# Squares of A's first block moved from the first pass to the third and fifth late pair, B's first squares all on ScalarE, and a new instruction order, in a 4096³ matmul with GELU

## The chip, the cores and the metric

The kernel runs on one core of one Trainium2 chip. The metric is device time in microseconds (us) of one launch. The profiled execution gives each engine's span in addition: TensorE (PE, with its weight loads PEld), VectorE (DVE), ScalarE (ACT), GpSimd (POOL, which issues the loads that cast f32 to f16) and SyncE (SP, which issues the stores).

## The reference

```python
def setup_inputs():
    m, k, n = 4096, 4096, 4096
    return {"a": np.random.randn(m, k).astype(np.float32),
            "b": np.random.randn(k, n).astype(np.float32)}

def reference(a, b):
    x = np.matmul(a, b)
    return 0.5 * x * (1 + np.tanh(np.sqrt(2 / np.pi) * (x + 0.044715 * x**3)))
```

## The kernel before, in words

**Tiling.** The product is computed in f16 with a seven-product scheme (Strassen and Winograd) instead of eight. A and B are cut into quadrants 11, 12, 21, 22. A *group* is one pair (mb, nb): 512 rows of each half of A by 512 columns of each half of B, over the whole depth of 4096; there are 16 groups. Group 0 (`first_group`) computes the first half of its depth with eight plain products, while the inputs still arrive, and the second half with seven. Groups 1 to 3 (`raw_group`, `last_raw`) use seven products P1 to P7. The other twelve groups run as six *late pairs* (`late_pair`, `ga` = 4, 6, 8, 10, 12, 14), where each product is split by the same scheme once more (`split_pair`). The third and fifth late pair are `ga` = 8 and 12. PE runs all products in one fixed sequence.

**Where things lie.** SBUF tiles: `aT` holds the transposed quadrants of A, `bR` eight chunks for quadrants of B and their sums, `aD` four chunks for sums of A, `stage` two chunks for rows as loaded, `y` small f32 blocks, `acc` the eight PSUM banks. In group 0, `bR_73/74` are the two depth halves of B12, `bR_75/76` of B22, `bR_77/78` of B21, `bR_79/80` of B11. Loads of f32 inputs go through POOL's queue and are cast on the way; sums of B that later groups need again are stored by SP (`k_unit`) and fetched by POOL.

**The check.** f16 is only used if no row of A and no column of B is too large or too small: the kernel sums squares of A's rows into `stats["a"]` and of B's columns into `stats["b"]`, and at the end `final_checks` and `verdict` decide whether `general_path` must run. For A's first block the squares are taken as each chunk is loaded in `load_a_`: sixteen `weigh0` activations per chunk (L684, `weigh_row`), written to a junk buffer with the row sum beside it; `weigh_first_half` adds the parts. The later blocks of A are squared in `turn_quad` (L1359, `weigh`). B's squares are 1024-wide pieces: `square` makes them on ACT (L1408) or on DVE (L1405), as the table `SQ` says for the four quadrants of group 0's first half, and DVE adds them up in bf16 (L1413). The pieces go through spare buffers: in group 0 one `y` block and the four halves of `bR_78`, the chunk that B21's second half is loaded into later.

**What sets the order.** All work after the first two products is recorded in a `Plan` as operations with an engine, a cost, what they read and write, and a slack. A planner with a table of costs (`COST`, `EVERY`, `MOVE`, `WEIGHT`) puts each engine's operations in order; `EARLIER` shifts due times of single operations, and `AFTER` is a list of moves "put operation n right behind m" made on the planner's result. Each engine then runs its list strictly in that order, so a waiting instruction holds what stands behind it.

```python
SQ = {"12": True, "11": True, "22": False, "21": True}   # True: on DVE
...
            for r in range(NX):                            # in load_a_, 16 rows of a chunk
                act("weigh0", lambda r=r: weigh_first(quad, cc, (r,), next(junk)), toks,
                    [("w0",), ("rows", 0), ("rows", 1)],
                    batch=("w0", quad, cc), slack=FIRST_SLACK)
```

The line numbers in the profile are those of the kernel; L964 (`combine2`: sums of A or B chunks on DVE), L1322 (`add_bank`: PSUM plus a block), L656 (`transpose`), L838 (`dma`), L744 and L1972 (the products), L1316 and L2384 (copies out of and between banks on ACT) are helpers that many steps share.

Of the kernel before, what the change touches and what calls it, by code (L numbers as in the profile page):

```python
# [18 lines left out]
Q = 32  # L19
# [33 lines left out]
UNDER_WAY = {"POOL": [(0.68, 12.2)] * 4}  # L53
# [2470 lines left out]
```

## Time and profile before

| | |
|---|---|
| median of 3 runs | 1445.19 us (1443.98 to 1448.59) |
| profiled execution, its own time | 1448.0 us |
| its span (first to last instruction) | 1446.4 us |
| PE busy | 1419.4 us, 98% of the span |
| DVE busy | 1238.0 us, 86% |
| ACT busy | 692.1 us, 48% |
| POOL busy | 487.5 us, 34% |
| moved by DMA | 380.99 MB; 339.74 MB read from HBM |

PE works nearly all the time, so what can be gained or lost lies in the few places where it waits, most of them in the first 130 us. The page's busy shares are averages; the stages differ: in group 0 the inputs arrive at about 200 GB/s (counted on the f16 side), and in the late pairs the DMA engines have room.

### The profile page before, as it was taken

What the parts mean: (1) busy time and instruction counts of PE and PEld (TensorE: products, weight loads), DVE (VectorE), ACT (ScalarE), POOL (GpSimd) and SP (SyncE); (2) the same over time, 40 slices, a digit from 0 to 9 for tenths busy, and PEclk for the clock granted to TensorE, in tenths of its full rate; (3) what the DMA queues carried; (4) which work ended last, traced back from release to release, by engine and by line L of the source; (5) the groups of instructions that cost most, each with busy time, mean ns of one, the idle gap of its engine ahead of it and who ended that gap; (6) DMA issues with size and microseconds to landing.
All of it is one profiled execution on the core that took longest, in us unless ns stands there. A gap on an engine that the chain in (4) does not pass through costs nothing. (4 is left out here: it accounts for less than half of the span.)

```text
span 1446.4 us, 19351 instructions
## 1 busy us (share of the span) xinstructions
PE 1419.4 (98%) x6707; PEld 656.3 (45%) x6707; DVE 1238.0 (86%) x1331; ACT 692.1 (48%) x1492; POOL 487.5 (34%) x892
## 2 busy tenths in 40 slices
PE   8989999999999999999999999999999999999998
PEld 3434455465444444444444444444444444444443
DVE  2997797998889999979897988887998998878876
ACT  4966656358866313543655313353463622333133
POOL 6554245054225152324423342332322231231220
PEclk9999999999999999999999999999999999999999
DMA  9999999999999998989979897998998967796773
GB/s 171 203 241 272 311 298 266 338 237 271 295 299 248 335 201 231 310 276 276 321 259 318 274 216 270 257 248 276 280 348 241 302 160 228 273 313 217 260 256 140
DMA packets 207674, 380.99 MB, mean 263 GB/s; under 512 B 20944, under 2 KB 119760, under 8 KB 207568
## 3 DMA queue, kind: packets, MB, share of 16 engines
q0 software_dynamic: 150400, 247.52, 71.7%
q1 hardware_dynamic: 57168, 132.15, 24.4%
q8 instruction: 55, 0.90, 0.2%
q14 instruction: 51, 0.42, 0.1%
HBM read 339.74 MB, written 134.22 MB: 328 GB/s over the span
## 5 line engine op out<-in xcount | busy, mean ns | idle before, releaser
L1972 PE MATMUL acc<-bR 128*128 128x512 f16 x1568 | 346.8, 379 | 0.4 <-DVE bR L964 0.2
L1972 PEld LDWEIGHTS <-bR 128*128 128x128 f16 x1984 | 193.9, 98 | 235.0 <-DVE bR L964 1.3
L1972 PE MATMUL acc<-bR,aT 128*128 128x512 f16 x1280 | 283.4, 379 | 4.8 <-DVE bR L964 3.9
L1972 PEld LDWEIGHTS <-aT 128*128 128x128 f16 x1664 | 162.6, 98 | 202.0 <-issue 6.2
L838 POOL DMA_DIRECT2D bR<-k_unit x224 | 121.4, 545 | 367.9 <-PE acc L1972 265.2
L964 DVE TENSOR_TENSOR bR<-bR 128x4096 f16<-128x4096 f16 (+1 forms) x114 | 210.6, 1858 | 29.6 <-PE acc L1972 20.3
L838 POOL DMA_DIRECT2D bR<-in_b_dram x320 | 173.6, 546 | 159.0 <-DMA bR<-in_b_dram 61.3
L1984 ACT COPY acc<-acc 128x512 f32<-128x512 f32 x168 | 95.7, 574 | 274.7 <-PE acc L1972 247.4
L1322 DVE TENSOR_TENSOR y<-acc,y 128x512 f32<-128x512 f32 x269 | 177.1, 685 | 25.1 <-PE acc L1972 24.2
L1972 PE MATMUL acc<-bR,aD 128*128 128x512 f16 x736 | 163.6, 379 | 0.0
L1296 ACT ACTIVATE y<-y 128x512 f32<-128x512 f32 x174 | 105.3, 625 | 112.2 <-DVE y L1322 111.9
L1972 PEld LDWEIGHTS <-aD 128*128 128x128 f16 x1024 | 100.2, 98 | 120.8
L744 PE MATMUL acc<-bR,aT 128*128 128x512 f16 x544 | 119.9, 379 | 2.2 <-DVE y L1322 1.2
L744 PEld LDWEIGHTS <-aT 128*128 128x128 f16 x768 | 75.1, 98 | 92.3 <-issue 3.3
L1981 ACT COPY y<-acc 128x512 f32<-128x512 f32 x114 | 66.4, 585 | 94.5 <-PE acc L1972 87.1
L1408 ACT ACTIVATE y<-bR 128x1024 bf16<-128x1024 f16 x83 | 84.9, 1051 | 36.5 <-DVE y L1413 33.8
L838 POOL DMA_DIRECT2D stage<-in_b_dram x104 | 56.3, 546 | 121.9 <-PE acc L1045 32.3
L744 PEld LDWEIGHTS <-aD 128*128 128x128 f16 x608 | 59.4, 98 | 77.9 <-DVE aD L964 4.2
L1972 PE MATMUL acc<-stage,bR 128*128 128x512 f16 x416 | 94.0, 379 | 0.0
L1413 DVE TENSOR_TENSOR y<-y 128x1024 bf16<-128x1024 bf16 x102 | 70.0, 688 | 25.6 <-ACT y L1408 24.0
L1972 PE MATMUL acc<-stage,aT 128*128 128x512 f16 x384 | 86.8, 379 | 0.0
L1327 DVE TENSOR_TENSOR acc<-acc,y 128x512 f32<-128x512 f32 x115 | 78.9, 693 | 5.3 <-ACT y L1981 5.0
(128 smaller groups left out, 1769.0 us busy)
## 6 DMA issues: line engine op xcount, KB each, us to landing
bR<-k_unit POOLq DMA_DIRECT2D x224, 512.0 KB, 7.8
out_dram<-y SPq DMA_DIRECT2D x194, 256.0 KB, 6.8
bR<-in_b_dram POOLq DMA_DIRECT2D x328, 128.0 KB, 7.0
k_unit<-bR SPq DMA_DIRECT2D x78, 512.0 KB, 7.0
stage<-k_unit POOLq DMA_DIRECT2D x60, 512.0 KB, 7.0
bR<-in_a_dram POOLq DMA_DIRECT2D x64, 256.0 KB, 9.2
k_unit<-stage SPq DMA_DIRECT2D x30, 512.0 KB, 8.0
out_dram<-bR SPq DMA_DIRECT2D x56, 256.0 KB, 6.7
```

Source lines behind the costliest of these rows:

```text
L744: nc.tensor.matmul(acc, sa[:, j // 2, i * P : (i + 1) * P, j % 2], sb[:, j, :], start=start and j == 0, stop=stop and j == 3, skip_group_c ...
L838: return plan.add(queue, COST[queue], lambda: eng.dma_start(out=dst, in_=src), r=r, w=w, size=MOVE[what] * SPREAD, weight=weight, **kw)
L964: nc.vector.tensor_tensor(out=dst, in0=xa, in1=ya, op=ALU.add if op > 0 else ALU.subtract)
L1296: act("gelu", lambda: nc.scalar.activation(t, t, ACT.Gelu_apprx_tanh), [("f", f)], [("f", f)])
L1322: dve("add", lambda: nc.vector.tensor_tensor(out=sm(g), in0=bank(s, i), in1=sm(f), op=ALU.add), [("f", f)], [("f", g), ("p", s, i)])
L1327: dve("add", lambda: nc.vector.tensor_tensor(out=bank(s, i), in0=bank(s, i), in1=sm(f), op=ALU.add), [("f", f)], [("p", s, i)])
L1408: act("square", lambda t=t, src=src: nc.scalar.activation(t, src, ACT.Square), [c(cx)], [("f", f)], slack=60.0, lead=lead)
L1413: dve("add16", lambda t=t, u=u: nc.vector.tensor_tensor(out=u, in0=u, in1=t, op=ALU.add), [("f", f)], [("f", e)], slack=60.0, lead=lead)
L1972: nc.tensor.matmul(bank(w, i), sa[:, jx // 2, r * P : (r + 1) * P, jx % 2], bv[:, jx, :], start=p in "17" and jx == 0, stop=jx == NJ - 1, ...
L1981: act("copy", lambda: nc.scalar.copy(out=sm(f), in_=bank(w, i)), [("p", w, i)], [("f", f)])
L1984: act("copy", lambda: nc.scalar.copy(out=bank(*dst), in_=bank(*x)), [("p", *x)], [("p", *dst)])
```

## The change

1. `load_a_` and the first steps no longer square A's rows: the 128 `weigh0` activations, `weigh_row`, `weigh_first` and `weigh_first_half` are gone.
2. A new `weigh_again` reads the rows of A's first block a second time: eight sets, each four loads through POOL into a free chunk, eight in-place `weigh` activations, and after every fourth set one small reduction on DVE. `AGAIN` puts the sets at the products P6, P5, P3 and P4 of the late pairs 8 and 12. A gate ties the loads to a PE operation nine before the place in PE's sequence.
3. `SQ` is False for all quadrants: the twelve squares that DVE made in group 0 are made by ACT.
4. `EARLIER`, `AFTER` and the planner's costs are new, so the order of DVE, ACT, POOL and SP changes from the first loads on. PE's sequence of products is the same; from the third late pair on some operands lie in other chunks.

```diff
-UNDER_WAY = {"POOL": [(0.68, 12.2)] * 4}
+UNDER_WAY = {"POOL": [(0.68, 13.2)] * 4}
...
-SQ = {"12": True, "11": True, "22": False, "21": True}
+SQ = {'12': False, '11': False, '22': False, '21': False}
...
+AGAIN = {8: {'P6': ('11', 0), 'P5': ('11', 1), 'P3': ('12', 0), 'P4': ('12', 1)}, 12: {'P6': ('21', 0), 'P5': ('21', 1), 'P3': ('22', 0), 'P4': ('22', 1)}}
+AGAIN_SLACK = 20.0
...
+    def weigh_again(quad, h, x0):
+        ih, kh = int(quad[0]) - 1, int(quad[1]) - 1
+        n = NX // 2
+        s, toks, t = chunk(x0).rearrange("p (x r) -> p x r", r=CH * RUN), [c(x0), c(x0 + 1)], rows_again[ih]
+        gate = [o for o in plan.ops if o.eng == "PE"][-CAST_BACK:][:1]
+        for g in range(4):
+            dma("POOL", s[g * Q : (g + 1) * Q, :, :], a_v[kh, g, :, ih * MH // Q + h * n : ih * MH // Q + (h + 1) * n, :],
+                [], toks, "raw_a", batch=("again", quad, h), slack=AGAIN_SLACK, after=gate)
+        for x in range(n):
+            r = h * n + x
+            act("weigh", lambda x=x, r=r: nc.scalar.activation(
+                s[:, x, :], s[:, x, :], ACT.Square, accum_out=t[:, kh, r : r + 1]),
+                [], [("again", ih), *toks], batch=("wa", quad, h), slack=SLACK)
+        if kh and h:
+            dve("small", lambda: nc.vector.tensor_reduce(
+                out=stats["a"][:, ih * NX : (ih + 1) * NX], in_=t.rearrange("p k x -> p x k"), axis=AX.X, op=ALU.add,
+            ), [("again", ih)], [("sa", 0, ih)], slack=60.0)
...
+        again = dict(AGAIN.get(ga, {}))
+
         def both(name, fresh, done):
+            if name in again:
+                x = new_chunk()
+                weigh_again(*again.pop(name), x)
+                free_cells.extend((x, x + 1))
...
-            for r in range(NX):
-                act("weigh0", lambda r=r: weigh_first(quad, cc, (r,), next(junk)), toks,
-                    [("w0",), ("rows", 0), ("rows", 1)],
-                    batch=("w0", quad, cc), slack=FIRST_SLACK)
...
-        dve("stat", weigh_first_half, [("w0",)], [("sa", 0, 0), ("sa", 0, 1)], slack=300.0)
```

**Loads in group 0.** POOL's queue from the first load of B11's first half (`bR_79`) on, before. `stage_87` receives A21, `stage_86` A12, `aD_82` A22 (first halves); `bR_75` is B22, `bR_77` B21:

```order
L838 DMA bR_79<-in_b_dram 32x4x512 x5
L838 DMA stage_87<-in_a_dram 32x16x256
L838 DMA bR_79<-in_b_dram 32x4x512 x3
L838 DMA stage_87<-in_a_dram 32x16x256
L838 DMA bR_75<-in_b_dram 32x4x512
L838 DMA stage_86<-in_a_dram 32x16x256
L838 DMA stage_87<-in_a_dram 32x16x256 x2
L838 DMA stage_86<-in_a_dram 32x16x256 x2
L838 DMA bR_77<-in_b_dram 32x4x512 x2
```

The same place in the change:

```order
L913 DMA bR_79<-in_b_dram 32x4x512 x8
L913 DMA stage_87<-in_a_dram 32x16x256 x4
L913 DMA stage_86<-in_a_dram 32x16x256
L913 DMA bR_75<-in_b_dram 32x4x512
L913 DMA stage_86<-in_a_dram 32x16x256 x3
L913 DMA bR_77<-in_b_dram 32x4x512 x3
```

All of B11 now goes ahead of A21, and all of A21 ahead of B22 and A12. Further down the queue, before, up to the last load of B21's first half (`bR_77`):

```order
L838 DMA bR_77<-in_b_dram 32x4x512 x2
L838 DMA bR_75<-in_b_dram 32x4x512 x3
L838 DMA aD_82<-in_a_dram 32x16x256 x2
L838 DMA bR_75<-in_b_dram 32x4x512 x4
L838 DMA aD_82<-in_a_dram 32x16x256 x2
L838 DMA stage_87<-in_a_dram 32x16x256 x4
L838 DMA bR_77<-in_b_dram 32x4x512 x4
```

and in the change, where `bR_74` and `bR_80` are second halves of B12 and B11:

```order
L913 DMA bR_80<-in_b_dram 32x4x512
L913 DMA bR_75<-in_b_dram 32x4x512 x4
L913 DMA bR_80<-in_b_dram 32x4x512
L913 DMA bR_74<-in_b_dram 32x4x512 x2
L913 DMA bR_77<-in_b_dram 32x4x512
L913 DMA bR_80<-in_b_dram 32x4x512 x2
L913 DMA bR_77<-in_b_dram 32x4x512 x3
L913 DMA aD_82<-in_a_dram 32x16x256 x4
```

The last load of B21 stood behind eight loads of A22 and of A11's second half; now four loads each of `bR_74` and `bR_80` stand ahead of it instead, and A22 comes behind it.

**DVE in the second half of group 0**, before, up to the transposes of A12's second half (`aT_68`). L1413 are the additions of B's squares:

```order
L1322 TENSOR_TENSOR y_98<-acc_107,y_98 128x512
L1413 TENSOR_TENSOR y_97<-y_97,bR_78 128x1024
L1322 TENSOR_TENSOR y_99<-acc_108,y_99 128x512
L1413 TENSOR_TENSOR y_97<-y_97,y_102 128x1024
L1322 TENSOR_TENSOR y_90<-acc_109,y_90 128x512
L1322 TENSOR_TENSOR y_100<-acc_109,y_100 128x512
L1413 TENSOR_TENSOR y_97<-y_97,bR_78 128x1024
L1413 TENSOR_TENSOR y_96<-y_96,bR_78 128x1024
L1413 TENSOR_TENSOR y_97<-y_97,bR_78 128x1024
L1322 TENSOR_TENSOR y_91<-acc_110,y_91 128x512
L1322 TENSOR_TENSOR y_101<-acc_110,y_101 128x512
L656 STREAM_TRANSPOSE aT_68<-stage_87 128x4x256 x2
```

The same place in the change:

```order
L1039 TENSOR_TENSOR bR_74<-bR_76,bR_74 128x2048
L1397 TENSOR_TENSOR y_98<-acc_107,y_98 128x512
L1039 TENSOR_TENSOR bR_74<-bR_76,bR_74 128x2048
L1039 TENSOR_TENSOR aT_72<-aT_66,aT_72 128x2048
L1397 TENSOR_TENSOR y_91<-acc_110,y_91 128x512
L1397 TENSOR_TENSOR y_89<-acc_108,y_89 128x512
L1397 TENSOR_TENSOR y_90<-acc_109,y_90 128x512
L1397 TENSOR_TENSOR y_99<-acc_108,y_99 128x512
L1397 TENSOR_TENSOR y_100<-acc_109,y_100 128x512
L752 STREAM_TRANSPOSE aT_68<-stage_87 128x4x256
L1397 TENSOR_TENSOR y_101<-acc_110,y_101 128x512
L752 STREAM_TRANSPOSE aT_68<-stage_87 128x4x256
```

No addition of squares is left there. Between the first transpose of `aT_72` and the first of `aT_68` the list held twelve L1413 and two L1405 before, and holds four L1413 (now L1509) in the change; the last of them that reads `bR_78` stands before the second `aD_81` sum.

**Loads in the third late pair.** POOL in the change, around the loads of P3 from the input (`bR_74`, `bR_73`, `stage_87`, `bR_75`); the `in_a_dram` rows are the rows of A read again, `k_unit_241` a cast of B made for a later pair:

```order
L913 DMA bR_73<-in_a_dram 32x8x512 x4
L913 DMA bR_78<-k_unit_218 128x2048
L913 DMA stage_86<-k_unit_234 128x2048 x2
L913 DMA bR_78<-k_unit_218 128x2048
L913 DMA k_unit_241<-in_b_dram 32x4x512
L913 DMA bR_77<-k_unit_218 128x2048
L913 DMA bR_74<-in_b_dram 32x4x512 x2
L913 DMA bR_77<-k_unit_218 128x2048
L913 DMA bR_74<-in_b_dram 32x4x512 x4
L913 DMA bR_73<-in_b_dram 32x4x512 x4
L913 DMA bR_74<-in_b_dram 32x4x512
L913 DMA bR_73<-in_b_dram 32x4x512 x2
```

Before, the queue there held, after the casts and the fetches of P5's sums, only P3's loads:

```order
L838 DMA stage_87<-k_unit_250 128x2048 x2
L838 DMA bR_73<-k_unit_234 128x2048
L838 DMA k_unit_257<-in_b_dram 32x4x512
L838 DMA bR_73<-k_unit_234 128x2048
L838 DMA stage_86<-in_b_dram 32x4x512
L838 DMA bR_75<-k_unit_250 128x2048 x2
L838 DMA stage_86<-in_b_dram 32x4x512 x2
```

Ten loads of A now go ahead of the last of P3's 32 loads, and three of the sixteen casts, all ahead of it before, behind it.

More of the change, by code (lines that the diff above doesn't have):

```diff
@@ L1 @@
 from contextlib import ExitStack
-from itertools import cycle
 import concourse.bass as bass
@@ L60 @@
 MOVE = {
-    "store": 1.345, "fetch": 1.38, "quarter": 1.6, "piece": 1.27, "out": 0.73, "raw_a": 1.3, "raw_b": 0.645,
-    "raw_a0": 1.363, "raw_b0": 0.64, "tiny": 0.2, "out_half": 0.3,
+    "store": 1.31, "fetch": 1.291, "quarter": 1.6, "piece": 1.27, "out": 0.743, "raw_a": 1.304, "raw_b": 0.649,
+    "raw_a0": 1.377, "raw_b0": 0.6444, "tiny": 0.2, "out_half": 0.3,
 }
 WEIGHT = {
-    "raw_a0": 1.31, "raw_b0": 1.06, "store": 2.0, "fetch": 2.42, "quarter": 2.16, "piece": 2.16, "raw_a": 1.11,
-    "raw_b": 1.06, "out": 1.05,
+    "raw_a0": 1.263, "raw_b0": 1.13, "store": 2.06, "fetch": 2.18, "quarter": 2.16, "piece": 2.16, "raw_a": 1.22,
+    "raw_b": 0.98, "out": 1.14,
 }
@@ L299 @@
 LEAD12 = 0.0
+LEAD11 = 500.0
 LEAD22 = 0.0
@@ L680, in load @@
             nc.gpsimd.dma_start(out=dst, in_=src)
-    def weigh_row(dst, src, to=None):
-        nc.scalar.activation(src if to is None else to, src, ACT.Square, accum_out=dst)
-    def weigh_first(quad, c, xs, to=None):
-        ih, kh = int(quad[0]) - 1, int(quad[1]) - 1
-        for x in xs:
-            k = ((kh * CH + c) * 2 + ih) * NX + x
-            weigh_row(stats["a"][:, k : k + 1], staged[quad, c][:, x, :], None if to is None else to[:, :])
-    def weigh_first_half():
-        t = tallies[:, 4 * NX : 6 * NX]
-        nc.vector.tensor_reduce(
-            out=t, in_=stats["a"].rearrange("p (k x) -> p x k", k=2 * CH), axis=AX.X, op=ALU.add
-        )
-        nc.vector.tensor_copy(out=stats["a"][:, : 2 * NX], in_=t)
     def gather(s):
@@ L792, in half_path @@
     before = {}
-    for n, whats in ((0, "A11_0a B12_0a A11_0b B12_0b T11_0a T11_0r T11_0s W11_0"),):
+    for n, whats in ((0, "A11_0a B12_0a A11_0b B12_0b T11_0a T11_0r T11_0s"),):
         for what in whats.split():
             half = what[-1] == "0" and what != "A11_0"
-            if what[0] == "W":
-                before.setdefault(n, []).append((weigh_first, (what[1:3], int(what[4]), range(NX))))
-                continue
             for h in (0, 1) if half else (None,):
@@ L1331, in half_path @@
     next_stage = [0]
-    rows = [tallies[:, 2 * ih * NX : 2 * (ih + 1) * NX].rearrange("p (k x) -> p k x", k=2) for ih in range(2)]
+    rows, rows_again = (
+        [tallies[:, 2 * k * NX : 2 * (k + 1) * NX].rearrange("p (k x) -> p k x", k=2) for k in (2 * n, 2 * n + 1)]
+        for n in range(2)
+    )
     seen_rows = set()
@@ L2316, in first_group @@
         SPARES[0][:] = [14, *spares_1]
-        load_b_("11", 0)
+        load_b_("11", 0, LEAD11)
         load_a_("21", 0)
```

4 lines of the change are left out of this document (2 added, 2 removed), and 416 rows, old and new, of tables (AFTER, EARLIER).

## The prediction

> **What bounds the kernel now.** I read the page first, then the list of whom PE waits for, PE's own timeline at those waits, and then, stage by stage, DVE, POOL and the two DMA queues. The page's span and busy shares:
>
> ```profile
> span 1446.4 us, 19351 instructions
> PE 1419.4 (98%) x6707; PEld 656.3 (45%) x6707; DVE 1238.0 (86%) x1331; ACT 692.1 (48%) x1492; POOL 487.5 (34%) x892
> ```
>
> PE is idle for 1446.4 - 1419.4 = 27.0 us, and PE's sequence of products isn't changed, so the change can gain at most part of these 27 us. The list of PE's waits (us in total, times, longest):
>
> ```profile
> PE acc L2260 <- DMA bR<-in_b_dram: 4.5, 3, 2.9
> PE acc L744 <- DVE aD L964: 4.4, 3, 1.9
> PE acc L1972 <- DVE bR L964: 4.1, 3, 2.4
> PE acc L744 <- DVE stage L964: 2.1, 2, 1.8
> PE acc L773 <- DVE aT L656: 1.6, 1, 1.6
> PE acc L753 <- DVE table L811: 1.5, 1, 1.5
> PE acc L744 <- DVE y L1322: 1.2, 1, 1.2
> PE acc L744 <- ACT acc L2384: 1.0, 1, 1.0
> PE acc L1972 <- DMA bR<-in_b_dram: 0.8, 1, 0.8
> PE acc L1972 <- DMA bR<-k_unit: 0.2, 1, 0.2
> ```
>
> They sum to 21.4 us; the other 5.6 us are the tail behind the last product. L753 and L773 (3.1 us, before the first data are there) keep their order, as does the tail. L2260, aD and ACT acc (9.9 us) are group 0; "stage" (2.1) is group 1; the L1972 rows and y (6.3) come later. PE's timeline, with its wait ahead of each piece in brackets:
>
> ```profile
> 14.87 5.45 PE L773 MATMUL acc<-bR,aT 128*128 128x512 f16 x24 [1.59 <-DVE aT L656]
> 23.20 27.16 PE L2260 MATMUL acc<-bR,aT 128*128 128x512 f16 x118 [2.88 <-DMA bR<-in_b_dram]
> 54.48 20.66 PE L2260 MATMUL acc<-bR,aT 128*128 128x512 f16 x95 [0.95 <-DMA bR<-in_b_dram]
> 115.70 7.07 PE L744 MATMUL acc<-aD,aT 128*128 128x512 f16 x32 [1.17 <-DVE aD L964]
> 180.32 7.07 PE L744 MATMUL acc<-stage,aD 128*128 128x512 f16 x32 [1.85 <-DVE stage L964]
> 863.99 7.08 PE L1972 MATMUL acc<-bR,aT 128*128 128x512 f16 x32 [2.38 <-DVE bR L964]
> ```
>
> **The change, part by part.** *The loads at the start.* PE waits 2.88 us for B11's first half (`bR_79`). Whole loads of A are 262 KB on the f16 side; the two queues in 30 to 80 us carry, in MB and in share of 16 engines:
>
> ```profile
> q0 software_dynamic: 14921, 9.56, 130.1%
> q1 hardware_dynamic: 144, 0.52, 2.8%
> ```
>
> That is 9.56 + 0.52 MB in 50 us, about 0.20 MB per us, so a load of A takes 1.3 us and one of B 0.65 us. One load of A, ahead of the last three of `bR_79` before, now stands behind: the product can start 1.3 us earlier. The wait also cost clock. The stretches behind it (last columns: granted clock, DMA share, GB/s):
>
> ```profile
> 24.00:26.00 2.00, 2.00 (x6) 0.76 (x5) 0.00 (x0) 0.00 (x0) 1.16 (x2) 0.50 1.42 195
> 26.00:28.00 2.00, 2.00 (x10) 0.87 (x9) 0.00 (x0) 0.00 (x0) 0.59 (x2) 0.92 1.44 198
> ```
>
> Half speed from 23.2 to 26 and a little after lost some 1.5 us; the 1.59 us wait at 13.3 lost none. With a wait of 1.6 us I expect none, so 2.8 us in all. The next product needs A21, whose last load has one load of B and one of A less ahead of it, 0.65 + 1.3 = 1.95 us; this caps the gain, so I take 2.0 us (0 if transfers in flight share evenly and nothing lands earlier, 2.8 at most). The Trainium skill ("TensorE: Matmul & The Clock Gate", Part 1) has the clock fall only after an idle window of about 3.4 us; by it the 2.88 us wait would not have lost 1.5 us, and the sum for this place would be 1.3 us; the trace shows the loss.
>
> PE's other two waits for B in group 0 (4.5 - 2.9 = 1.6 us) are for B21's first half: 56 units of 0.65 us stood up to its last load, now 48, which is 5.2 us earlier; 1.6 us go (0 to 1.6). A22, now behind it, comes 12 units (7.8 us) later. Its transposes began here:
>
> ```profile
> 46.51 2.37 DVE L656 STREAM_TRANSPOSE aT<-aD 128x1024 uint32<-128x1024 uint32 x2 [1.33 <-DMA stage<-in_a_dram]
> ```
>
> so they come at about 54, and its product is the one behind the waits that end at 54.5, each product of 32 matmuls taking 7 us: it stays covered by that product, and if the cover goes, up to 1.6 us come back.
>
> *Squares off DVE and ACT in group 0.* DVE in 63 to 111 us (after the window's length stand the busy us of PE, PEld, DVE, ACT and POOL), and the additions of squares among its groups in 30 to 130 us:
>
> ```profile
> 63.00:111.00 48.00, 43.75 (x202) 19.42 (x200) 47.40 (x59) 33.51 (x117) 26.00 (x48) 1.00 1.23 231
> ...
> L1413 DVE TENSOR_TENSOR y<-y,bR 128x1024 bf16<-128x1024 bf16 x18 | 12.1, 683 | 0.2
> ```
>
> DVE is full there (47.4 of 48), and PE's three waits for `aD` lie in it. The order takes 12 + 2 squares and additions in this stretch down to 4: ten instructions of 12.1/18 = 0.67 us, 6.7 us. That covers the 4.4 us of waits. ACT's 128 squares of rows, which stood between its copies, go too:
>
> ```profile
> L684 ACT ACTIVATE stat_b<-stage x40: 399/406/433, 30.0 to 106.9; 128x256 f16<-128x256 f16 x40
> L1408 ACT ACTIVATE bR<-bR x9: 1040/1050/1057, 51.6 to 93.2; 128x1024 bf16<-128x1024 f16 x9
> ```
>
> At least 128 x 0.41 = 52 us leave, 12 x 1.05 = 12.6 us come, so PE's 1.0 us wait for ACT can go. Together 5.4 us (2 to 5.4: sums that now run early may wait for the chunks they need, and hold DVE's list).
>
> The front's sum is 2.0 + 1.6 + 5.4 = 9.0 us at 116 us.
>
> *What the transfers give back.* Group 1's sums wait for the last of its B: DVE at 179 us. POOL in 130 to 190 us waits nearly always for earlier loads to land (us, times, longest). Then the queues' shares in 80 to 180, q1 alone in 183 to 188, and both in 180 to 430 us:
>
> ```profile
> 179.04 1.23 DVE L964 TENSOR_TENSOR stage<-bR,stage 128x2048 f16<-128x2048 f16 x1 [1.80 <-DMA bR<-in_b_dram]
> ```
>
> ```profile
> POOL bR L838 <- DMA bR<-in_b_dram: 16.5, 18, 1.4
> ```
>
> ```profile
> q0 software_dynamic: 12540, 10.69, 67.9%
> q1 hardware_dynamic: 6128, 17.14, 46.6%
> ...
> q1 hardware_dynamic: 568, 2.06, 102.3%
> ...
> q0 software_dynamic: 25834, 25.47, 60.5%
> q1 hardware_dynamic: 15904, 46.31, 49.3%
> ```
>
> A full q0 shows 130% and a full q1 102%. So 80 to 180 us are filled to 67.9/130.1 + 46.6/102.3 = 0.98: 2.3 us are free. Removing squares removes no transfer; the loads group 1 needs, and the stores ahead of them, are the same in number. So of 9.0 us I let PE keep 2.3 us at its product at 180 us; the rest shows up as a longer wait there, now 2.1 us. The bounds are 0 (no free time can be used) and 9.0 (stores slip behind the loads).
>
> *Behind 180 us.* The 6.3 us of later waits are each short of one late chunk or one sum; every list is ordered anew. DMA has 1 - 60.5/130.1 - 49.3/102.3 = 0.05 free in 180 to 430 us. No row prices a new order; between 6.3 us gained and 3 us lost (another wait as long as the 2.38 us at 861 us) I take the half, 3.1 us.
>
> *Rows read again.* 32 loads of 1.3 us are 41 us of transfer, 64 squares, at the durations of the later blocks' squares,
>
> ```profile
> L1359 ACT ACTIVATE stage<-stage x64: 612/617/656, 643.9 to 1144.4; 128x512 f16<-128x512 f16 x64
> L1359 ACT ACTIVATION_READ_ACCUMULATOR stage<-stage x64: 185/189/214, 644.4 to 1144.9; 128x1 f32 x64
> ```
>
> at most 64 x 0.81 = 52 us of ACT, in two of the six late pairs. ACT is 48% busy over the span, and PE's list has no wait for such squares, which ran in the second and fourth pair. POOL issues 32 more loads; it is 34% busy. The cover is thin only where pair 8 waits for P3's loads; DVE there, and the queues in 814 to 864 us:
>
> ```profile
> 861.65 2.29 DVE L964 TENSOR_TENSOR bR<-stage,bR 128x4096 f16<-128x4096 f16 x1 [3.26 <-DMA stage<-in_b_dram]
> ```
>
> ```profile
> q0 software_dynamic: 5998, 8.88, 85.0%
> q1 hardware_dynamic: 1008, 1.84, 9.7%
> ```
>
> 85.0/130.1 + 9.7/102.3 = 0.75, so 12.6 of 50 us are free. Ahead of P3's last load come ten loads of A more (13.0 us) and three casts less (1.9 us): 11.1 us. It fits if spread; I take 0.5 us (0 to 11).
>
> **Sum.** -2.3 - 3.1 + 0.5 = -4.9 us. The profiled execution took 1448.0 us (span 1446.4 and 1.6 around it), 0.2% over the median; from it 1443.1, from the median 1445.2 - 4.9 = **1440.3 us**.
>
> **Rivals.**
>
> 1. *The front's gain stays.* If transfers can overlap better than the shares say, all 9.0 us remain: 9.0 + 3.1 - 0.5 = 11.6, 1433.6 us. For it: some stretches were not full, such as this one, with its 216 GB/s:
>
> ```profile
> 100.00:105.00 5.00, 5.00 (x25) 2.27 (x24) 4.94 (x7) 5.00 (x20) 2.99 (x6) 1.00 1.07 216
> ```
>
> Against it: the fill of 0.98, and POOL waiting for landings 18 times.
> 2. *Nothing stays.* The transfers take back all of the front, and the later waits only change places: 0 to 2 us, about 1444 us. For it: the same fill; group 1 ends when its last load lands. The Trainium skill ("DMA: Bandwidth & Descriptors", Issuing engines are not separate DMA queues) says that DMAs of all issuers end up on the same 16 engines and interleave, so a load issued earlier meets the same stores; here q0 and q1 do add up to one full share.
> 3. *Slower: the rows read again hold up P3 in pair 8.* The ten loads meet P3's in the last part of the stretch up to the sum at 861 us, where only part of the 12.6 us is free. All 11.1 us late in pair 8 and 2 us in pair 12 cost 13, less the 5.4 of front and order: 1452.8 us. It is slower by 0.3% (4.3 us, about what a measurement can tell) only from 9.7 us on, when the 2.4 us wait becomes 12. Against it: eight of the ten stand ahead of P3's first load in POOL's list.
>
> **Chances.** My forecast 0.45, rival 1 0.17, rival 2 0.25, rival 3 0.13. My forecast's own range is 1437 to 1443; a little over half (0.28) lies under 1440.85, which is 0.3% faster. Faster 0.28 + 0.17 = 0.45, same 0.17 + 0.25 = 0.42, slower 0.13. The range 1433.5 to 1447.5 leaves out rival 3 and about half of rival 1.
>
> **What will show it.** Right: waits of L2260 under 2.5 us and a clock of 1.0 at 24 us; no wait for `aD` over 1 us; PE's wait for "stage" in group 1 grown from 2.1 to 6 us or more; the product of 180.3 us starting at 177 to 179. Rival 1: that product at 171 to 174. Rival 3: a wait over 5 us at the start of P3 in pair 8 (about 860 us). The forecast is wrong if group 0's DVE list stalls on late chunks, or if later waits, under the new order, exceed 9 us.

## The result, and the profile after

The changed kernel took 1462.36 us (median of 4 runs, 1457.87 to 1464.11) against 1444.88 us of the kernel before beside it: ratio 1.011, 95% interval 1.0092 to 1.0129. That is 13 to 19 us slower, where 4.9 us less were forecast. Its profiled execution took 1462.97 us. The page's span and busy shares, then some of PE's waits (us in total, times, longest):

```profile
span 1461.3 us, 19125 instructions
PE 1424.8 (98%) x6707; PEld 656.6 (45%) x6707; DVE 1225.1 (84%) x1319; ACT 684.4 (47%) x1376; POOL 506.6 (35%) x924
```

```profile
PE acc L2068 <- DVE bR L1039: 8.8, 6, 2.6
PE acc L822 <- DVE aD L1039: 8.4, 1, 8.4
PE acc L822 <- DVE stage L1039: 2.1, 1, 2.1
PE acc L822 <- DVE bR L1039: 1.8, 1, 1.8
PE acc L2357 <- DMA bR<-in_b_dram: 1.6, 1, 1.6
```

DVE and ACT have less to do, as the change says. PE is idle for 1461.3 - 1424.8 = 36.5 us instead of 27.0, and busy 5.4 us longer for the same products. About 4 us of these are time at half clock: PE is busy for 11.0 us at half clock here (86.69 to 90.93, 169.44 to 172.86, 1319.75 to 1323.15) and for 3.1 us in before (23.20 to 26.33), and half of that is lost. The waits for B's first loads (L2260 before, L2357 now) fell from 4.5 to 1.6 us; one wait of 8.4 us for `aD` stands in place of three that came to 4.4, and the waits for late `bR` sums of the later products (L1972 before, L2068 now) come to 8.8 us instead of 4.1. PE's timeline, with the wait ahead of each piece in brackets:

```profile
21.72 48.55 PE L2357 MATMUL acc<-bR,aT 128*128 128x512 f16 x224 [1.59 <-DMA bR<-in_b_dram]
71.22 7.08 PE L822 MATMUL acc<-bR,aT 128*128 128x512 f16 x32 [0.95 <-DVE aT L752]
86.69 9.16 PE L822 MATMUL acc<-aD 128*128 128x512 f16 x32 [8.40 <-DVE aD L1039]
...
481.15 7.07 PE L2068 MATMUL acc<-bR,aT 128*128 128x512 f16 x32 [1.96 <-DVE bR L1039]
...
873.65 7.07 PE L2068 MATMUL acc<-bR,aT 128*128 128x512 f16 x32 [2.07 <-DVE bR L1039]
...
1319.75 12.18 PE L2068 MATMUL acc<-bR 128*128 128x512 f16 x48 [2.57 <-DVE bR L1039]
```

The same two products as at 71.22 and 86.69, in before:

```profile
75.08 7.07 PE L744 MATMUL acc<-bR,aT 128*128 128x512 f16 x32
81.99 7.07 PE L744 MATMUL acc<-aD 128*128 128x512 f16 x32
```

PE is 3.9 us ahead at the first and 4.7 late at the second: 8.6 us are lost between two neighbours. What lies behind the wait of 8.40 us is seen in three steps: DVE at 77.67 waits for rows of A (the second half of A21); SP had issued four stores at 62.8 to 65.0; and in 68 to 74 us these stores (q1) hold the DMA engines while the loads (q0) crawl.

```profile
77.67 1.25 DVE L752 STREAM_TRANSPOSE aT<-aD 128x1024 uint32<-128x1024 uint32 x1 [5.94 <-DMA aD<-in_a_dram]
```

```profile
62.80 0.34 SPq L913 DMA_DIRECT2D k_unit<-aD  x1
63.30 0.92 SPq L913 DMA_DIRECT2D k_unit<-bR  x1
64.26 0.69 SPq L913 DMA_DIRECT2D k_unit<-aD  x1
65.00 0.60 SPq L913 DMA_DIRECT2D k_unit<-bR  x1
```

```profile
q1 hardware_dynamic: 500, 1.83, 81.1%
q0 software_dynamic: 530, 0.26, 31.7%
```

```profile
aD<-in_a_dram POOLq DMA_DIRECT2D x4, 256.0 KB, 15.0
stage<-in_a_dram POOLq DMA_DIRECT2D x4, 256.0 KB, 15.8
```

The last fence gives the DMA issues of 60 to 80 us with the median us from issue to landing; the same kind of load took 6.6 us in before, and the very loads of `aD` take 7.9 us in e1 below:

```profile
stage<-in_a_dram POOLq DMA_DIRECT2D x4, 256.0 KB, 6.6
```

**A ledger.** The table compares the profiled executions by the start of the same product: start in PE's timeline less the start of that matmul, counted along PE's sequence, in before (us; minus is ahead; some records are missing, so it is good to about 0.4 us). The columns are before's times. The kernels e1 to e12 are those of the next section.

| kernel | 53 | 82 | 116 | 180 | 284 | 402 | 473 | 785 | 1306 | end |
|---|---|---|---|---|---|---|---|---|---|---|
| after | -3.8 | +4.7 | +0.8 | +3.5 | +2.1 | +5.1 | +8.4 | +8.6 | +13.7 | +15.4 |
| e1 | -3.3 | -2.4 | -6.3 | -2.6 | -4.0 | -1.6 | 0.0 | +4.1 | +8.9 | +8.9 |
| e2 | -3.3 | +3.3 | 0.0 | +0.9 | -0.5 | +5.4 | +6.3 | +7.5 | +13.0 | +13.0 |
| e3 | -2.4 | +4.6 | +1.2 | +2.1 | +4.8 | +7.8 | +8.2 | +8.5 | +16.0 | +16.0 |
| e4 | +0.4 | +0.6 | 0.0 | -2.1 | -2.8 | +1.3 | +5.9 | +5.2 | +4.8 | +4.8 |
| e5 | -3.1 | -2.3 | -6.2 | -2.5 | -3.9 | -2.8 | +4.4 | +7.9 | +11.5 | +11.5 |
| e6 | -3.4 | -1.7 | -5.3 | -3.7 | -5.0 | +2.4 | +6.0 | +5.6 | +5.6 | +5.6 |
| e7 | -3.5 | -2.0 | -5.9 | -8.3 | -9.7 | -3.1 | -1.6 | -2.8 | +1.0 | +1.0 |
| e8 | -0.6 | +1.1 | -0.8 | -1.3 | -1.6 | -0.8 | -2.0 | -2.9 | -4.0 | -4.0 |
| e9 | -3.4 | -2.9 | -6.8 | -5.9 | -7.2 | -5.5 | -4.7 | -5.3 | -1.0 | -1.0 |
| e10 | -2.9 | -2.1 | -5.9 | -4.6 | -5.9 | +0.3 | +1.8 | +3.2 | +3.2 | +3.2 |
| e11 | -2.9 | 0.0 | -2.5 | +0.9 | -0.5 | +6.5 | +6.4 | +6.0 | +6.0 | +6.0 |
| e12 | -2.5 | -2.0 | -5.9 | -5.2 | -6.6 | -1.2 | +1.1 | +4.1 | +4.6 | +4.6 |

For the changed kernel it shows four losses: 8.5 us between 53 and 82, 2.7 between 116 and 180, 6.3 between 284 and 473, 6.8 from 785 on. The kernels with the new lists vary by 6 to 18 us from run to run (e1: 1449.92 to 1462.95), before by 5 to 11 on one chip (1440.68 to 1452.13 on e1's), so one execution's row is not the median, and medians decide below where they differ. The early stores, the first experiment's matter, show in every execution: at 116 us the eight kernels that hold four stores back (e1, e5 to e7, e9 to e12) are 2.5 to 6.8 us ahead, the three that don't and have the new front (the change, e2, e3) 0.0 to 1.2 us late.

### The profile page after: what moved, and what is told of

Same layout as the page of the kernel before. It is cut to its first block, busy times and chain, and to the rows that moved or that the text cites. A ratio compares the mean times of both kernels' runs of the same rounds, so it can differ in the third digit from the quotient of the medians.

```text
span 1461.3 us, 19125 instructions
## 1 busy us (share of the span) xinstructions
PE 1424.8 (98%) x6707; PEld 656.6 (45%) x6707; DVE 1225.1 (84%) x1319; ACT 684.4 (47%) x1376; POOL 506.6 (35%) x924
## 4 chain that ended last, share of the span: by engine, by line
PE 58%; DMA 14%; DVE 4%; issue 3%; POOL 1%; ACT 0%; SPq 0%; DVEq 0%; POOLq 0%; ACTq 0%
PE acc L2068 57%; DMA bR<-in_b_dram 5%; DMA bR<-in_a_dram 3%; DMA bR<-k_unit 3%; DVE bR L1039 2%; DMA stage<-k_unit 1%; PE acc L822 1%; POOL bR L913 1%; DMA k_unit<-bR 1%; DMA out_dram<-y 1%; DVE y L1397 1%; PE acc L1120 1%; DMA stage<-in_a_dram 1%; DVE y L1509 0%; DMA stage<-in_b_dram 0%
## 5 line engine op out<-in xcount | busy, mean ns | idle before, releaser
L2068 PE MATMUL acc<-bR 128*128 128x512 f16 x1344 | 300.2, 380 | 3.1 <-DVE bR L1039 2.9
L2068 PE MATMUL acc<-bR,aT 128*128 128x512 f16 x1280 | 284.2, 379 | 5.9 <-DVE bR L1039 5.0
L2068 PEld LDWEIGHTS <-bR 128*128 128x128 f16 x1824 | 178.5, 98 | 221.9 <-issue 5.9
L2068 PEld LDWEIGHTS <-aT 128*128 128x128 f16 x1664 | 162.6, 98 | 203.9 <-DMA bR<-in_b_dram 2.8
L913 POOL DMA_DIRECT2D bR<-in_b_dram x336 | 182.2, 545 | 188.1 <-DMA bR<-in_b_dram 31.4
L913 POOL DMA_DIRECT2D bR<-k_unit x210 | 114.0, 546 | 333.2 <-PE acc L2068 199.6
L1039 DVE TENSOR_TENSOR bR<-bR 128x4096 f16<-128x4096 f16 (+1 forms) x107 | 194.8, 1828 | 24.7 <-PE acc L2068 9.1
L2068 PE MATMUL acc<-bR,aD 128*128 128x512 f16 x752 | 167.4, 379 | 1.4 <-DVE aD L1039 0.9
L2068 PEld LDWEIGHTS <-aD 128*128 128x128 f16 x1024 | 100.1, 98 | 122.8 <-DVE aD L1039 1.4
L1504 ACT ACTIVATE y<-bR 128x1024 bf16<-128x1024 f16 x86 | 88.5, 1052 | 56.4 <-DVE y L1509 52.4
L2068 PE MATMUL acc<-stage,bR 128*128 128x512 f16 x480 | 108.0, 379 | 0.9 <-DVE bR L1039 0.9
L913 POOL DMA_DIRECT2D bR<-in_a_dram x108 | 63.2, 590 | 95.7 <-ACT y L1437 46.4
L1509 DVE TENSOR_TENSOR y<-y 128x1024 bf16<-128x1024 bf16 x102 | 69.8, 686 | 23.1 <-ACT y L1504 21.6
L1402 DVE TENSOR_TENSOR acc<-acc,y 128x512 f32<-128x512 f32 x115 | 76.7, 693 | 13.8 <-ACT y L2077 13.7
L2068 PE MATMUL acc<-stage,aT 128*128 128x512 f16 x384 | 86.8, 379 | 0.4 <-DMA stage<-k_unit 0.4
```

Source lines behind the costliest of these rows:

```text
L913: return plan.add(queue, COST[queue], lambda: eng.dma_start(out=dst, in_=src), r=r, w=w, size=MOVE[what] * SPREAD, weight=weight, **kw)
L1039: nc.vector.tensor_tensor(out=dst, in0=xa, in1=ya, op=ALU.add if op > 0 else ALU.subtract)
L1402: dve("add", lambda: nc.vector.tensor_tensor(out=bank(s, i), in0=bank(s, i), in1=sm(f), op=ALU.add), [("f", f)], [("p", s, i)])
L1504: act("square", lambda t=t, src=src: nc.scalar.activation(t, src, ACT.Square), [c(cx)], [("f", f)], slack=60.0, lead=lead)
L1509: dve("add16", lambda t=t, u=u: nc.vector.tensor_tensor(out=u, in0=u, in1=t, op=ALU.add), [("f", f)], [("f", e)], slack=60.0, lead=lead)
L2068: nc.tensor.matmul(bank(w, i), sa[:, jx // 2, r * P : (r + 1) * P, jx % 2], bv[:, jx, :], start=p in "17" and jx == 0, stop=jx == NJ - 1, ...
```

## The experiments

**e1: the four stores held back.** The stores of group 0's first kept sums wait until the second half of A22 is transposed:

```diff
 HOLD = {
+    215: 125,
     1645: 1568,
```

> The changed kernel, with the first four stores of kept sums on SP (0.5 MB each) waiting on the chip until the last rows of A22 are transposed; nothing else moves. In the changed kernel they go out at 62.8 to 65.0 us, q1 has 80% of the engines from 68 to 74 us, and A's loads, 6.6 us before, take 15 us. Theory A (these four stores delay the loads that DVE waits 5.9 us for): the wait of 8.4 us ahead of the product at 86.7 us is under 1.5 us, no half clock there (2.3 us), and the product that started at 116.5 us starts 8 to 11 us earlier; total 1462 less 6 to 11, so 1451 to 1456. Theory B (the traffic as a whole is too much, the stores only show where): A's loads land as late as before, or the wait moves to the products at 152 and 168 us; 1459 to 1464.

1455.54 us; ratio 1.0065 (1.0038 to 1.0092), where the change has 1.011. SP, PE, and the loads' queue in 68 to 74 us:

```profile
78.31 0.34 SPq L914 DMA_DIRECT2D k_unit<-aD  x1
```

```profile
79.60 7.10 PE L823 MATMUL acc<-aD 128*128 128x512 f16 x32 [2.00 <-DVE aD L1040]
97.36 5.34 PE L823 MATMUL acc<-bR,aT 128*128 128x512 f16 x24 [2.03 <-ACT acc L2482]
...
146.47 8.75 PE L823 MATMUL acc<-bR,aT 128*128 128x512 f16 x32 [2.33 <-DMA bR<-in_b_dram]
163.92 20.88 PE L823 MATMUL acc<-stage,aD 128*128 128x512 f16 x96 [1.79 <-DVE stage L1040]
```

```profile
q0 software_dynamic: 2364, 1.17, 144.9%
```

The wait of 8.40 is now 2.00 us, and the loads move 1.17 MB in these 6 us instead of 0.26. The early stores are shown as the first cause: 1462.36 - 1455.54 = 6.8 us of the median (the ratios' intervals make it good to some 5 us), and 7.1 us in the ledger at 116 us. The product at 116 us now starts 6.3 us early, and 3.7 of these are gone at 180: PE waits for B at 146.47 and for group 1's sums at 163.92.

**e2: the check's verdict later.** In the change DVE waits for the gathered sums of squares shortly before PE's wait at 1319.75:

```profile
1314.35 0.31 DVE L789 TENSOR_REDUCE verdict<-bR 1x1 f32<-1x128 f32 x1 [7.70 <-DMA bR<-seen_d]
```

SP issued that read at 1308.3 us, behind the stores of kept sums; before at 1283.4. e2 puts the verdict behind a later DVE operation:

```diff
 AFTER = [
+    (4270, 4325),
```

> The changed kernel, with the check's last step on DVE (the verdict, which waited 7.7 us at 1306 us for two rows read back) moved behind nine more instructions of DVE. Theory A (this step in DVE's list causes PE's wait of 2.57 us at 1319.75 and the half clock behind it): both go, 1462 less 3.5 to 4.5, so 1457.5 to 1458.5. Theory B (the stores of kept sums on SP ahead are late anyway, and the sums behind the step wait for something else): 1461 to 1464.

1461.07 us; 1.0107 (1.008 to 1.0134). In its profile the product starts without a wait, at 1318.99. In the change the lag grows by 4.4 us at that place, the wait and the half clock behind it, and in e1, e7 and e9, which keep the verdict's old place, by 2.0, 1.9 and 1.0. But e2's execution lost more than the change's elsewhere, and its median, 1.3 us lower, can't be told from the change's: the wait has gone, and what it costs by medians isn't settled.

**e3 and e4: the lists behind 180 us exchanged.** e3 is the change with before's order of the operations numbered 600 to 2700 (the second half of group 1 to about 765 us); e4 is before with the changed kernel's order there. Both by a table applied to the planner's result:

```diff
+        for e, ids in FIXED.items():
+            s, nxt = set(ids), iter(ids)
+            order[e] = [self.ops[next(nxt)] if o.n in s else o for o in order[e]]
```

> The changed kernel, but from the second half of group 1 to the pair at 596 to 765 us each engine takes its steps in the order of the kernel before (same steps, same tiles; 945 of 3100 steps move). The changed kernel lost 5.0 us against the kernel before between 187 and 765 us (its lag grew from 3.5 to 8.5 us). Theory A (the order made anew costs this): 3 to 6 us faster, 1456 to 1459. Theory B (the lag is the front's late loads carried on, or chance of the profiled execution): within 2 us of 1462.

> The kernel before, but in the same stretch each engine takes its steps in the changed kernel's order; front, squares and the pairs from 765 us on are those of before. Theory A (the new order costs 5 us there by itself): 1448 to 1451. Theory B (the new order is no worse, the lag comes from the front): 1443 to 1447.

e3: 1462.49 us, 1.0106 (1.0088 to 1.0125), no better than the change. e4: 1454.74 us, 1.0059 (1.0041 to 1.0077): nothing else of the change is in it, so a new order there is enough to lose 6 to 11 us of the median, more than the forecast (at most 3 lost) or the first theory (5) had. In its profile it all comes between 284 and 473 us (8.7 us). But e3 shows that the old order is no cure in the new surroundings: it lost 2.7 us between 180 and 284, part of it where the two orders meet, and 3.4 between 284 and 473.

**e5 and e6: the order mended at one sum, and the rows not read again.** e5 is e1 with two moves: e2's, and one sum into `bR`, which PE waited for at 407 us in the change, stands further ahead. e6 is e5 without the 32 loads (the squares run on what lies in the chunks, and the second block's sums stand in for theirs):

```diff
+    (4270, 4325), (1436, 1327),
...
+        if len(self.ops) in SKIP:
+            fn = lambda: None
```

The first line is e5's; the other two are e6's, where `SKIP` lists the 32 loads.

> As e1 (the changed kernel, its first four stores held until A22 is transposed; 1455.5 us), with two steps of DVE's list moved: the sum that PE waited for at 407 us goes ahead of a transpose that stood 4.9 us waiting for its rows, and the check's verdict nine instructions later. Theory A (DVE's list, not the data, makes PE wait in these two places): no wait there, 1.8 and 2 us less, 1451 to 1453. Theory B (the lists behind fit only within a microsecond or two, and what is gained at one place is waited for at the next): 1454 to 1457.

> As e5, but the 32 loads that read the first block's rows once more are not issued (the 64 squares run on what lies in the tiles, and their sums are replaced by the second block's), so it prices the loads alone. Theory A (the loads, 8.4 MB in two pairs, delay other loads): e5 less 2 to 5 us. Theory B (they fit in free transfer time, as forecast with 0.5 us): within 1.5 us of e5.

e5: 1457.24 us, 1.008 (1.0048 to 1.0112), no faster than e1, as its second theory had it. The wait at 407 is gone, and two others stand behind it:

```profile
404.64 1.89 PE L824 MATMUL acc<-bR,aT 128*128 128x512 f16 x8 [1.83 <-DVE y L1399]
...
477.13 9.96 PE L2070 MATMUL acc<-bR,aT 128*128 128x512 f16 x32 [3.16 <-DVE bR L1041]
```

e6: 1451.96 us, 1.0042 (1.0027 to 1.0057), 5.3 us under e5 on the same chip, though the two intervals overlap. From 785 us on its lag doesn't grow, and in e10 to e12, also without these loads, by 0.5 us at most, while e5's grows by 3.6, e1's by 4.8 and the change's by 6.8. Of the last two, 2.0 and 4.4 come at the product of e2, where e5, e6 and e10 to e12 have e2's move and no wait. That leaves 2.4 to 3.6 us for the loads in these three executions (5.5 in e2's own), none of it in one place, and 5.3 by medians. The two DMA queues of the change in 785 to 1190 us, then the loads' queue of e6, where the other shows 15.7%:

```profile
q0 software_dynamic: 42954, 89.81, 83.2%
q1 hardware_dynamic: 12384, 23.60, 15.5%
```

```profile
q0 software_dynamic: 36923, 83.66, 74.4%
```

**e7: 16 output stores of group 0 left out**, 4.2 MB, to see whether the transfers take the front's gain back; else as e1.

```diff
+SKIP = {266, 327, 328, 329, 348, 351, 354, 357, 406, 407, 408, 409, 410, 411, 412, 413}
...
+        if len(self.ops) in SKIP:
+            fn = lambda: None
```

> As e1, but the 16 stores of the first group's results (4.2 MB, about 12 us of transfer between 109 and 190 us) are not issued. In e1 PE is 6.3 us ahead of the kernel before at 116 us and 2.6 us ahead at 180 us, with new waits of 2.3 us for a load of B at 146 us and 1.8 us for a sum behind such a load at 164 us. Theory A (the transfers give the front's gain back): these two waits go, PE is 5.5 us or more ahead at 180 us, total 1455.5 less 2 to 4. Theory B (the order of loads, not their amount, sets these waits): both waits stay within 1 us, 1454 to 1457.

1453.20 us, 1.0064 (1.0038 to 1.0089). In its profile the waits at 146 and 164 us are gone and PE is 8.3 us ahead at 180 where e1 has 2.6; between 284 and 473 it loses 8.1 again, with this wait first:

```profile
366.11 36.40 PE L826 MATMUL acc<-bR,aD 128*128 128x512 f16 x160 [3.10 <-DVE aD L1043]
```

The other kernels that hold the four stores and keep the output stores stand at 180 us between 5.9 ahead and 0.9 late, so this one execution supports that the transfers take back the front, without giving its size. A front that is 6 us further ahead is not seen at the end by the ratios (1.0064 against e1's 1.0065, each good to about 4 us).

**e8: the start alone.** Before, with B11's eight loads first in POOL's list and the next nine in the change's order.

```diff
+FIXED = {"POOL": [1, 5, 7, 4, 3, 2, 6, 0, 10, 11, 9, 8, 50, 75, ...]}
```

> The kernel before, with one part of the change alone: on POOL the eight loads of B11's first half stand first, ahead of the first block of A21 and of the loads behind (17 loads in the changed kernel's order, the rest as before). Forecast's term (a): the wait of 2.88 us at 20.3 us falls to 1.6 us, the clock stays at 1.0 behind it, PE is 2 to 2.8 us ahead at 24 us, and 1.5 to 3 us ahead at 75 us. Theory A (the transfers take it back by 180 us): 1444.5 to 1446.5. Theory B (it stays): 1443 to 1444.5. Against the forecast: less than 1 us ahead at 24 us.

1445.35 us against 1444.8, 1.0002 (0.9992 to 1.0011): no change. PE is 1.2 us ahead at the first product and 2.4 by 52 us, as forecast, and pays at the next load: it waits there for 2.46 us, runs at half clock from 54.32 to 57.73, and is 1.1 us late at 75:

```profile
22.04 28.05 PE L2269 MATMUL acc<-bR,aT 128*128 128x512 f16 x128 [1.58 <-DMA bR<-in_b_dram]
52.55 0.39 PE L2269 MATMUL acc<-bR,aT 128*128 128x512 f16 x1 [2.46 <-DMA bR<-in_b_dram]
```

It also shows that a disturbance at the front alone doesn't bring the loss between 284 and 473 (-0.4 there).

**e9 and e10: half of the rows' squares.** e1, and e10 with e5's moves and without the re-read loads, each with the squares of A's later rows over half the columns, to see whether ACT holds the loads behind 284 us (POOL waits there 44.3 us for `y` in e1).

```diff
-    s[:, x, :], s[:, x, :], ACT.Square, ...
+    s[:, x, :RUN], s[:, x, :RUN], ACT.Square, ...
```

> As e1, but each square of a row of A on ACT takes half the row (256 of 512 elements, 0.2 us less for each of 448 squares). Between 284 and 473 us every kernel with the new lists has lost 4 to 11 us against the kernel before (e1: 4.0), and POOL waits 37 to 46 us there for ACT to release the rows of A, against 30 us before. Theory A (ACT's squares hold the rows' tiles, so the rows and what DVE makes of them come late): POOL's wait for ACT in 330 to 410 us falls under 32 us and the loss to under 2 us; 1455.5 less 2 to 6. Theory B (the lists as written, with one or two late loads ahead of a needed sum on DVE, whatever ACT does): the loss stays at 3 us or more, 1453 to 1457.

> As e9, with e5's two moves on DVE, and the 32 loads of rows read again left out as in e6 (1452.0 us). If the prices add (stores 6.9, loads read again 5.3, and what e9 shows for ACT's squares): e6 less what e9 gains on e1, 1446 to 1452, and no loss against the kernel before from 785 us on. If they don't add (what one part frees is waited for elsewhere): 1451 to 1455.

e9: 1454.72 us, 1.0071 (1.0044 to 1.0098); POOL's wait for these squares in 284 to 480 us hardly shrinks, and it is as long in before; e9, then before:

```profile
POOL bR L914 <- ACT y L1438: 43.5, 4, 15.6
...
POOL bR L838 <- ACT y L1359: 45.0, 5, 14.7
```

e10: 1450.71 us, 1.0032 (1.0014 to 1.005), within e6's interval. Between 284 and 473 us e9's execution, the fastest of its six, loses 2.5 us and e10's 7.7. ACT's squares don't carry the loss.

**e11 and e12: where in 284 to 473 us?** Both are e6 with pieces of before's order: e11 everything planned in 335 to 482 us on four engines, e12 only 19 instructions of DVE and 48 loads of POOL. The reason for e12 is read in DVE's rows of e6: at 368.07 a sum waits for a load, ahead of the `aD` sum PE waits for.

```profile
368.07 1.23 DVE L1044 TENSOR_TENSOR bR<-bR 128x2048 f16<-128x2048 f16 x1 [3.04 <-DMA bR<-in_b_dram]
369.21 1.22 DVE L1044 TENSOR_TENSOR aD<-aD,aT 128x2048 f16<-128x2048 f16 x1
```

```profile
370.49 37.51 PE L827 MATMUL acc<-bR,aD 128*128 128x512 f16 x160 [3.34 <-DVE aD L1044]
```

In before both `aD` sums stand ahead of it, and PE doesn't wait:

```profile
364.24 2.36 DVE L964 TENSOR_TENSOR aD<-aD,aT 128x2048 f16<-128x2048 f16 x2
367.99 1.23 DVE L964 TENSOR_TENSOR bR<-bR 128x2048 f16<-128x2048 f16 x1 [1.39 <-DMA bR<-in_b_dram]
```

```diff
+FIXED = {"DVE": [...], "POOL": [...]}                              # e12
+FIXED = {"DVE": [...], "POOL": [...], "ACT": [...], "SP": [...]}   # e11
```

> The kernel without the 32 reads for the check (e6, 1451.96 us, with its first block's sums still replaced by the second block's), in which only the instructions planned between 335 and 482 us (122 on VectorE, 161 on ScalarE, 87 on GpSimd, 54 on SyncE) stand in the order that the same instructions have in before. Theory A (the order made anew is what loses time in this stretch: waiting sums and late loads ahead of what TensorE waits for): the waits at 370 us (3.34 us, with the half clock behind it 2.8 us), 451, 459 and 479 us (1.86, 0.91, 2.00 us) shrink to about one wait of 1.5 us as in before; the product's lag against before grows by at most 4 us between 284 and 473 us, where e6 lost 11.0, and the median falls by 4 to 8 us, to 1444 to 1448 us. Theory B (the stretch loses because the loads and sums behind 284 us come late for what lies before it, in whatever order): the lag still grows by 8 us or more there, and the median is 1450 to 1454 us.

> The same kernel (e6), in which only two pieces stand in before's order: 19 instructions of VectorE planned between 353 and 372 us (the two aD sums ahead of the bR sum that waits for a load, and the two transposes of one A block the other way round), and 48 of GpSimd's loads planned between 410 and 475 us (the four loads of A's rows ahead of most of B's, the two stage loads where they were). Theory A1 (these two pieces carry the loss): the wait at 370 us (3.34 us) falls under 1 us, VectorE's wait of 3.93 us for bR<-in_a_dram at 448.9 us falls to about 1.7 as in before, and the lag grows by at most 6 us between 284 and 473 us; the median is 1446 to 1449.5 us. Theory A2 (the loss belongs to the whole stretch, since a wait that is taken away comes back at the next place, as with the one sum moved in e5): the wait at 370 us is gone but others take its place, the lag grows by 7 us or more, median 1450 to 1453 us.

e11: 1450.98 us, 1.0033 (1.0017 to 1.005). e12: 1456.28 us, 1.0065 (1.0047 to 1.0084), no faster than e6 and above both its theories. In e11 the lag grows by 7.0 us between 284 and 402 and by nothing (-0.1) between 402 and 473, where the kernels with the new lists lost 0.8 to 7.2 (the change 3.3) and e3, in the old order too, 0.4. So neither theory has it whole: the lag grows by 6.9 us in all, between their bounds of 4 and 8, and the median is in the second one's range. The loss comes where the old order begins, with loads that land late:

```profile
345.67 6.85 PE L864 MATMUL acc<-bR,aT 128*128 128x512 f16 x31 [1.40 <-DMA bR<-in_a_dram]
368.96 43.14 PE L864 MATMUL acc<-bR,aD 128*128 128x512 f16 x192 [2.63 <-DVE bR L1081]
```

In e12 the wait for `aD` at 370 is gone and another took its place 6 us earlier, as e12's second theory had it; e6's 1.86 us at 451.30 became 2.74 at 448.60:

```profile
364.52 39.90 PE L841 MATMUL acc<-bR,aD 128*128 128x512 f16 x176 [2.34 <-DVE bR L1058]
...
448.60 3.63 PE L2087 MATMUL acc<-bR,aT 128*128 128x512 f16 x16 [2.74 <-DVE bR L1058]
```

## Why the prediction was wrong, step by step

- **Start and B21's loads (2.0 + 1.6 us): right in the profile.** PE's first wait is 1.59 us and the clock stays at full speed behind it; at 75 us PE is 3.9 us ahead in the change and 4.6 in e1. By the rule of the Trainium skill that was weighed at this place ("TensorE: Matmul & The Clock Gate", Part 1), no clock would have been lost before; e8 and the change keep full clock with the shorter wait, so the trace's loss was real. As a gain of its own, e8 shows, the start is worth nothing: it needs the later loads to come earlier too.
- **"It stays covered by that product" (the first half of A22): right.** DVE transposes it from 54.98 us on, where about 54 was forecast, and PE runs without a wait from 21.72 to 70.27.
- **"That covers the 4.4 us of waits" (DVE and ACT relieved, 5.4 us): failed, and the stores are 6.8 us of it.** At 116 us the change is 0.8 us late, where 9.0 were to be gained. The step took DVE's load for all that the `aD` sums wait for. The sum that PE waits for at 86.69 is made of the second halves of A21 and A22, and the prediction follows neither these rows nor the stores. All 16 loads of the second halves of B12 and B11 now go ahead of the rows: POOL issues those of A21 from 59.73 us on, before from 49.32. The second halves of B also let the sums of P5 run 20 us earlier, at 59.81 instead of 79.82:

```profile
59.73 2.54 POOL L913 DMA_DIRECT2D aD<-in_a_dram  x4
59.81 1.23 DVE L1039 TENSOR_TENSOR aD<-bR 128x2048 f16<-128x2048 f16 x1 [0.49 <-DMA stage<-in_a_dram]
```

```profile
49.32 0.65 POOL L838 DMA_DIRECT2D aD<-in_a_dram  x1 [0.79 <-DMA stage<-in_a_dram]
79.82 1.22 DVE L964 TENSOR_TENSOR aD<-bR 128x2048 f16<-128x2048 f16 x1 [0.28 <-issue]
```

With these sums done, the four stores behind them in SP's list went out from 62.80 us on (before, one at 55.97 and three from 82.81), in front of A's rows. In `first_group` the planner ties them to the last load of A12's second half (`gate`), which POOL issues only from 84.13 us on: the tie stands in the plan and is no wait on the chip. The prediction named this sign of being wrong itself, group 0's DVE list stalling on late chunks; it is the 5.94 us at 77.67.
- **What the same term is worth without the stores: mis-sized, 1.7 of 5.4 us.** In e1 the ledger goes from -4.6 at 75 us to -6.3 at 116. PE still waits 2.00 us for `aD` and 2.03 for ACT's copies, which themselves wait for DVE (ACT idles 4.40 us ahead of those at 96.74); in 63 to 80 us DVE is as full as before (16.66 of 17.00 us).
- **The transfers give back the front: right in sign, and the size in part by luck.** Of the gain, 2.3 us were to be left at 180 us. The change, already late at 116, has none, 3.5 late; e1 has 2.6, but e5, e6, e9, e10 and e12, with the same front, 2.5 to 5.9, and e11 is 0.9 late. e7 speaks for transfers: without 4.2 MB of stores 8.3 are left. The place was wrong: PE's wait for `stage` was to grow to 6 us or more; it is 2.1 in the change, and e1 loses its time in two waits, for B at 146 and for `stage` at 164 us, and in half clock behind the first. The 130% taken for a full q0 is loose too: alone in 68 to 74 us of e1 it shows 144.9%.
- **Behind 180 us (3.1 us gained, bounds 6.3 gained to 3 lost): failed, and the largest error.** e4, which has only this, loses 6 to 11 us. "Another wait as long as the 2.38 us" took one wait for the bound. Before has one wait over 0.5 us between 360 and 480 us (1.48); the traces of the new lists have three or four, of 0.5 to 3.5 us, one behind the other, some with half clock behind them. The bound should have been their number times such a wait.
- **Rows read again (0.5 us, bounds 0 to 11): mis-sized, 5.3 us by the medians of e5 and e6, 2.4 to 5.5 by profiles.** Rival 3 had the sign, not the place: P3 in pair 8 waits 2.07 us against 2.38 before. It is spread: q0 rises by 9 points of the sixteen engines' time (83.2 against 74.4%). By the prediction's own scale the queues stay under full with it, 83.2/130.1 + 15.5/102.3 = 0.79 over these 405 us, so a mean fill below 1 didn't show that the loads fit.

By medians 6.8 + 5.3 + 8.5 (e4: 0.59% of 1445) are 20.6 us, and what the front keeps at 180 us, 2.6, leaves 18.0; measured are 17.5. The sum fits, but the terms are good to 3 to 5 us each and the third comes from another kernel's surroundings, so the fit proves little. **What stays open:** whether it is the new order as such that loses between 284 and 473 us, or any order that meets the loads at other times than it was fitted to. For the first speak e4, the stretch behind 402 us in e3 and e11, and one wait of 0.9 us at the same product (455.5 us in before) in all ten kernels with the new DVE list there and in none of the four with the old; for the second e3, e5, e11's own loss at its start and e12, where each mended wait came back next door. No hybrid with mixed lists was free of the loss, and only before and e8, whose lists behind 30 us are the same, were. The price of the verdict's place (e2) is not settled either.

## What to carry to other kernels

When loads are moved ahead, follow every operation whose last operand now lands earlier, down to the stores it frees: a store that nothing but its data holds back goes out at once, whatever the plan says, and here four of them took the DMA engines from the loads that were needed next (6.8 us). And where one engine is 98% busy and its feeders run fixed lists, allow for a price of a newly planned order (6 to 11 us in e4): count the places where one late load or sum can hold a list, and set the bound by their number, not by the longest wait seen so far.

## What the runs showed of the hardware

- **A burst of stores starves the casting loads.** In 68 to 74 us of the change q1 held 81.1% of the engines' time and q0 31.7%; the loads of `aD` took 15.0 us to land, and 7.9 in e1 without the burst. The queues moved about as many packets, 500 and 530, but 3.7 KB each against 0.5. The Trainium skill ("DMA: Bandwidth & Descriptors", Issuing engines are not separate DMA queues) says that DMAs of all issuers interleave on the same engines; the trace agrees, and adds that they don't do so evenly.
- **Half clock comes in pieces of 3.41 us and behind waits shorter than that.** The change runs at a granted clock of 0.50 from 80.7 to 90.9 us, three pieces. Waits of 2.06 us (at 168.29), 2.29 (e11 at 150.16), 2.33 (e1 at 146.47) and 2.57 (1319.75) were followed by one piece, about 1.6 us lost; such a row is the one of 8.75 us for 32 matmuls above. Waits of 2.07 (873.65), 1.96 (481.15) and before's 2.38 were not. The Trainium skill ("TensorE: Matmul & The Clock Gate", Part 1) gives a free-running window of 3413 ns, and the pieces agree with it; that a whole window has to be idle doesn't fit a loss behind 2.06 us. What tells them apart can be read from the traces: in each, the changes of the clock lie whole multiples of 3.413 us from one another (the change's second and third loss start 26 and 363 of them behind the first). On that grid, from 18 us to the last product of the fourteen traces, each of the 23 windows at full clock in which PE idled 1.98 us or more (the least is e10's at 144.06) was followed by half clock, and none in which it idled 1.93 us (e5 at 93.90) or less. The wait of 2.06 us lies in one window; before's 2.38 us is split, 0.99 and 1.39. The windows (us, busy us of PE, PEld, DVE, ACT and POOL, then granted clock, DMA share, GB/s), the change's two and before's three:

```profile
166.03:169.44 3.41, 1.35 (x7) 0.56 (x6) 2.32 (x3) 0.57 (x1) 1.15 (x3) 1.00 1.19 220
169.44:172.86 3.42, 3.42 (x10) 1.24 (x9) 3.32 (x5) 2.09 (x3) 0.48 (x1) 0.50 1.15 303
...
859.19:862.60 3.41, 2.42 (x12) 0.98 (x10) 0.95 (x1) 0.00 (x0) 0.89 (x2) 1.00 0.94 217
862.60:866.02 3.42, 2.03 (x10) 0.95 (x10) 3.42 (x4) 0.05 (x1) 0.00 (x0) 1.00 0.93 265
866.02:869.43 3.41, 3.41 (x18) 1.51 (x17) 3.41 (x3) 1.60 (x3) 0.00 (x0) 1.00 1.03 422
```
